# Transposing the sparse heads' attention weights as two 16-bit planes by DMA instead of by TensorE

## The chip, the cores and the metric

The kernel runs on one core of a Trainium2 chip. The metric is the device time of one execution in microseconds (us); below it is better. TensorE (PE) multiplies, VectorE (DVE) and ScalarE (ACT) work on whole tiles, GpSimd (POOL) does the rest, and SyncE (SP) issues most DMAs. Each engine takes its instructions in one fixed order.

## The reference

One layer of a hybrid block on 512 tokens of width 1024: a combined input projection, two attention branches of eight heads each (head size 64), sigmoid gates, an output projection, a layer norm, a gated MLP with a short causal convolution, and a second layer norm, all in float32. The change touches branch A, the sparse one:

```
dots  = einsum('thd,sd->ths', q_idx, k_idx) * IDX_DIM ** -0.5
score = einsum('th,ths->ts', w_idx, relu(dots))           # indexer
_, sel = top_k(where(key_chunk <= q_chunk, score, -inf), n_sel)   # n_sel = 128
logits = einsum('thd,tnhd->htn', qb, k[sel]) * HEAD_DIM ** -0.5 + rel_bias[t5_bucket(sel - t)]
p = softmax(where(valid, logits, -inf))
y_a = einsum('htn,tnhd->thd', p, v[sel])
...
merged = sigmoid(g_a) * (y_a @ w_branch_dsa) + sigmoid(g_b) * (y_s @ w_branch_sb)
```

## The kernel before

Float32 operands are split into a high and a low part of TensorE's own float32 format, and each product is three matmuls (high by high, high by low, low by high). `Stream` loads the weights in one fixed order as pieces of 128x1024 (512 KB, tile `raw`, three buffers) and splits them into `whi` (ACT) and `wlo` (DVE, some on POOL), three pieces ahead of their use.

The kernel's middle part works on 16 heads, first eight stick-breaking ones (s0 to s7), then eight sparse ones (a0 to a7). For each head `start_head` computes logits and weights; a sparse head does that in `dsa_head`. Keys run along the columns there, queries along the 128 partitions; the four query blocks j have 128(j+1) causal keys each, 1280 columns in all, which stand in one tile `lg` at the column offsets `OFF`. TensorE writes the logits to `l_ps`, DVE adds the bias and mask in `bm` and takes a row extreme (L493), ACT takes the exponential with its row sum (L495), DVE multiplies by the reciprocal (L501, four instructions).

The product with the values needs the weights with keys along the partitions. `turn_weights` does that: ten transposes of 128x128 per head on TensorE (L409, into `tr_ps`), then three copies on ACT to the high part `pth` (L413) and three subtractions on DVE to the low part `ptl` (L414). `weigh` multiplies these by the values in eight matmuls (L425, into `av_ps`); `avt`, `yat` and, for each pair of heads, `ya0h`/`ya0l` to `ya3h`/`ya3l` follow. Head i+1 is started before the weights of head i are turned. In the gaps `fill` puts the matmuls of projections that nothing waits for soon (`FILL`: the queries and keys of later heads, the gates `gb` and `ga`, the branch `bs`). One piece of 128x1024 gives 24 such matmuls. After the last head comes branch A's projection (`ba_ps`, L653 to L655), which needs `ya0` to `ya3`.

The written order is not the order on the engines: a scheduler places each instruction, from its own estimate of durations and what has been written first. Pools name a tag and its buffers; a tile waits until the one that had its buffer before has been read. `lg` has two buffers (tag `beta`, shared with the stick-breaking heads), `bm` two (tag `keep`), `pth` and `ptl` eight together (tag `pt`, shared with the indexer's tiles).

Of the kernel before, what the change touches and what calls it, by code (L numbers as in the profile page):

```python
# [21 lines left out]
NB = 4  # L22
# [94 lines left out]
def tile_block(ctx: ExitStack, tc: tile.TileContext, xT, xN, w_qi, w_ki, w_t, w_v, w_br, w_o, w_fi, w_fo,  # L117
# [226 lines left out]
    def idx_keys():  # L344
        ps = whole(proj_t("ki", M=72, bank=pa))
        kih = bp.tile([128, 512], F32R, tag="pt", bufs=8, name="kih")
        kil = bp.tile([128, 512], F32R, tag="pt", bufs=8, name="kil")
        wiT = bp.tile([8, 512], F32, tag="pt", bufs=8, name="wiT")
# [48 lines left out]


    def turn_weights(a):

        groups = (((0, 0),), ((1, 0), (3, 384)), ((2, 0),))
        pth, ptl = {}, {}
        for grp in groups:
            ps = pb("tr_ps")
            width = 0
            for i, o in grp:
# [3 lines left out]
                width = max(width, o + 512 - 128 * i)  # L410
            th = bp.tile([128, 512], F32R, tag="pt", bufs=8, name="pth")
            tl = bp.tile([128, 512], F32R, tag="pt", bufs=8, name="ptl")
            nc.scalar.activation(th[:, :width], ps[:, :width], AF.Copy)  # L413
            lows = nc.vector.tensor_sub(tl[:, :width], ps[:, :width], r32(th[:, :width]))  # L414
            for i, o in grp:
                pth[i] = th[:, o:o + 512 - 128 * i]
                ptl[i] = tl[:, o:o + 512 - 128 * i]
        return pth, ptl, lows.ins

    def weigh(pth, ptl, vt, h, ytmp):  # L420

        ps = pb("av_ps")
        seq = [(i, t) for i in range(NB) for t in (pth, ptl)]
        for n, (i, t) in enumerate(seq):
            nc.tensor.matmul(ps[:, 128 * i:512], vt[i][:, h].rearrange("p a d -> p (a d)"), t[i],  # L425
                             start=(n == 0), stop=(n == len(seq) - 1))
# [44 lines left out]
    def dsa_head(q, k, h):  # L471
# [4 lines left out]
        for j in (1, 2, 3):  # L476
            N = 128 * (j + 1)
            nc.gpsimd.tensor_add(bm[:, OFF[j]:OFF[j] + N], win[:, 512 - N:512], score[j])  # L478
        lg = bp.tile([128, ATT], F32, tag="beta", bufs=2, name="lg")
# [3 lines left out]
        for grp in ((3,), (0, 2), (1,)):  # L483
            ps = pb("l_ps")
            o = 0
            for j in grp:
                N = 128 * (j + 1)
                for hl in range(2):
                    nc.tensor.matmul(ps[:, o:o + N], q[:, hl, j * 128:j * 128 + 128], k[:, :N],
                                     start=(hl == 0), stop=(hl == 1))  # L490
                c = slice(OFF[j], OFF[j] + N)
                b = win[:, 384:512] if j == 0 else bm[:, c]
# [6 lines left out]
        for j in range(NB):  # L499
            c = slice(OFF[j], OFF[j] + 128 * (j + 1))  # L500
            nc.vector.tensor_scalar(lg[:, c], lg[:, c], rs[:, j:j + 1], None, op0=ALU.mult)  # L501
        return lg

# [81 lines left out]
    def start_head(i):  # L585
# [522 lines left out]
```

## Time and profile before

| | us |
|---|---|
| three runs | 764.51, 765.06, 765.46 |
| their median | 765.06 |
| span of the profiled execution | 765.6 |

The span runs from the first to the last instruction of the profiled execution. It is the only time that we have of that execution, and lies 0.5 us above the median. In the page, PE, DVE, ACT and POOL are the engines' busy times in the span, and the chain says which work ended last, followed back from the end. A row of the timeline has the start, the duration, the engine, the line and the operation; since matmuls are pipelined, what one costs is read from the distance of its start to the next start, not from its duration. A row of the groups has the count, the sum of the busy time and the mean of one, then the idle time just before and what ended it.

### The profile page before, as it was taken

To read this page: it belongs to the slowest core of one execution; us is meant where nothing else is said; L and a number is where in the kernel's file an instruction comes from. 1 tells how busy PE (TensorE), PEld (TensorE's weight loads), DVE (VectorE), ACT (ScalarE), POOL (GpSimd) and SP (SyncE) were. 2 spreads that over 40 slices of the span, in tenths; PEclk is the share of its full clock that TensorE was granted. 3 is DMA by queue.
4 is the path that set the end of the run, shared out by engine and by line. 5 is a ranking of instruction groups with operands and counts; after the bars stand their busy time and mean duration, and the time that the engine had idled before them with its cause. 6 is when DMAs were issued, how large, how long until landed. Compare 5 with 4: busy or idle time off the path is not lost.

```text
span 765.6 us, 9873 instructions
## 1 busy us (share of the span) xinstructions
PE 753.1 (98%) x3597; PEld 630.9 (82%) x3597; DVE 555.2 (73%) x908; ACT 365.0 (48%) x559; POOL 153.6 (20%) x160
## 2 busy tenths in 40 slices
PE   8999999999999999999999999999999999999995
PEld 6878888888888888888889888888888888888885
DVE  4559787799878585549855776867676758668994
ACT  5465656655474746836322434433443443346430
POOL 0002546426645210000101110111011101110021
PEclk9999999999999999999999999999999999999998
DMA  7436332232133323116801343433434443447641
GB/s 255 156 110 190 115 111 83 83 95 98 69 111 107 114 72 123 67 58 218 330 1 56 114 162 139 153 144 143 138 139 141 156 140 124 152 137 274 200 155 59
DMA packets 34112, 101.31 MB, mean 132 GB/s; under 512 B 4552, under 2 KB 4936, under 8 KB 34064
## 3 DMA queue, kind: packets, MB, share of 16 engines
q1 hardware_dynamic: 28336, 84.41, 31.6%
q0 software_dynamic: 3728, 11.04, 3.9%
q10 hardware_dynamic: 2000, 5.24, 2.7%
q8 instruction: 28, 0.46, 0.2%
q14 instruction: 20, 0.16, 0.1%
HBM read 88.59 MB, written 9.98 MB: 129 GB/s over the span
## 4 chain that ended last, share of the span: by engine, by line
PE 92%; DVE 5%; issue 1%; ACT 1%; DMA 1%; POOL 0%; POOLq 0%; SPq 0%; ACTq 0%; DVEq 0%
PE u_ps L746 5%; PE u_ps L747 5%; PE g_ps L746 5%; PE u_ps L745 5%; PE g_ps L747 5%; PE g_ps L745 5%; PE m L826 2%; PE m L825 2%; PE m L827 2%; PE av_ps L425 2%; PE ga_ps L223 2%; PE ga_ps L222 2%; PE ga_ps L224 2%; PE o_ps L703 2%; PE o_ps L702 2%; PE o_ps L704 2%
## 5 line engine op out<-in xcount | busy, mean ns | idle before, releaser
L100 ACT ACTIVATE whi<-raw 128x1024 fp32r<-128x1024 f32 (+1 forms) x124 | 124.1, 1001 | 169.5 <-PE g_ps L746 43.0
L102 DVE TENSOR_TENSOR wlo<-raw,whi 128x1024 fp32r<-128x1024 f32 (+1 forms) x105 | 120.0, 1143 | 44.0 <-ACT whi L100 41.1
L745 PE MATMUL u_ps<-x1h,whi 128*128 128x512 f32 (+1 forms) x192 | 71.4, 372 | 0.0
L747 PE MATMUL u_ps<-x1h,wlo 128*128 128x512 f32 (+1 forms) x192 | 71.4, 372 | 0.0
L746 PE MATMUL u_ps<-x1l,whi 128*128 128x512 f32 (+1 forms) x192 | 71.3, 371 | 0.0
L745 PE MATMUL g_ps<-x1h,whi 128*128 128x512 f32 (+1 forms) x184 | 69.9, 380 | 0.0
L746 PE MATMUL g_ps<-x1l,whi 128*128 128x512 f32 (+1 forms) x184 | 69.9, 380 | 0.0
L747 PE MATMUL g_ps<-x1h,wlo 128*128 128x512 f32 (+1 forms) x184 | 69.9, 380 | 0.0
L102 POOL TENSOR_TENSOR wlo<-raw,whi 128x1024 fp32r<-128x1024 f32 x19 | 45.8, 2412 | 34.4 <-ACT whi L100 34.4
L745 PEld LDWEIGHTS u_ps<-x1h,whi 128*128 128x128 f32 x192 | 36.2, 188 | 6.3
L746 PEld LDWEIGHTS u_ps<-x1l,whi 128*128 128x128 f32 x192 | 36.2, 188 | 6.2
L747 PEld LDWEIGHTS u_ps<-x1h,wlo 128*128 128x128 f32 x192 | 36.2, 188 | 6.2
L414 DVE TENSOR_TENSOR ptl<-tr_ps,pth 128x512 fp32r<-128x512 f32 (+1 forms) x48 | 27.9, 595 | 18.2 <-ACT pth L413 17.6
L745 PEld LDWEIGHTS g_ps<-x1h,whi 128*128 128x128 f32 x184 | 34.6, 188 | 6.6
L746 PEld LDWEIGHTS g_ps<-x1l,whi 128*128 128x128 f32 x184 | 34.6, 188 | 6.5
L747 PEld LDWEIGHTS g_ps<-x1h,wlo 128*128 128x128 f32 x184 | 34.6, 188 | 6.5
L768 DVE TENSOR_TENSOR t<-raw 128x512 f32<-128x512 f32 x11 | 7.6, 692 | 39.0 <-DMA raw<-in_w_fo_dram 39.0
L787 POOL MEMSET u<- 128x2 f32 x22 | 2.1, 98 | 150.5 <-ACT whi L100 99.5
L801 DVE TENSOR_TENSOR hF<-g_ps,c 128x512 f32<-128x512 f32 x22 | 15.1, 687 | 19.7 <-PE g_ps L747 18.9
L793 ACT ACTIVATE c<-c,cwt 128x512 f32<-128x512 f32 x22 | 15.9, 725 | 27.9 <-DVE c L792 27.7
L671 POOL TENSOR_TENSOR rstd<-rstd,mhalf 128x1 f32<-128x1 f32 x8 | 7.6, 951 | 105.5 <-DVE rstd L670 105.5
L478 POOL TENSOR_TENSOR bm<-win,score 128x256 f32<-128x256 f32 (+2 forms) x24 | 26.8, 1143 | 9.1 <-DVE mn L493 8.4
(562 smaller groups left out, 2047.9 us busy)
## 6 DMA issues: line engine op xcount, KB each, us to landing
raw<-in_w_fi_dram SPq DMA_DIRECT2D x44, 512.0 KB, 3.2
raw<-in_w_t_dram SPq DMA_DIRECT2D x32, 512.0 KB, 3.3
raw<-in_w_fo_dram SPq DMA_DIRECT2D x26, 512.0 KB, 4.0
raw<-in_w_br_dram SPq DMA_DIRECT2D x8, 512.0 KB, 3.2
raw<-in_w_o_dram SPq DMA_DIRECT2D x8, 512.0 KB, 4.0
raw<-in_w_v_dram SPq DMA_DIRECT2D x7, 512.0 KB, 3.7
raw_b<-in_w_fo_dram SPq DMA_DIRECT2D x6, 512.0 KB, 5.2
s_t<-t POOLq DMA_DIRECT2D x11, 256.0 KB, 2.3
```

Of the source, the lines that this page charges most:

```text
L100: nc.scalar.activation(hi[:, :w], t[:, :w], AF.Copy)
L102: self.done[key] = eng.tensor_sub(lo[:, :w], t[:, :w], r32(hi[:, :w])).ins
L222: nc.tensor.matmul(ps[:M], wh[:, c], xh[k], start=(k == 0), stop=False)
L223: nc.tensor.matmul(ps[:M], wh[:, c], xl[k], start=False, stop=False)
L224: nc.tensor.matmul(ps[:M], wl[:, c], xh[k], start=False, stop=(k == KC - 1))
L414: lows = nc.vector.tensor_sub(tl[:, :width], ps[:, :width], r32(th[:, :width]))
L425: nc.tensor.matmul(ps[:, 128 * i:512], vt[i][:, h].rearrange("p a d -> p (a d)"), t[i], start=(n == 0), stop=(n == len(seq) - 1))
L478: nc.gpsimd.tensor_add(bm[:, OFF[j]:OFF[j] + N], win[:, 512 - N:512], score[j])
L745: nc.tensor.matmul(ps[:, c], wh[:, kc], x1h[:, k, c], start=(k == 0), stop=False)
L746: nc.tensor.matmul(ps[:, c], wh[:, kc], x1l[:, k, c], start=False, stop=False)
L747: nc.tensor.matmul(ps[:, c], wl[:, kc], x1h[:, k, c], start=False, stop=(k == KC - 1))
L793: nc.scalar.activation(c, c, AF.Gelu_apprx_tanh, bias=cwt[:, f, 3:4])
```

## The change

The stick-breaking heads keep `turn_weights`. A sparse head now takes two functions. `send_planes`, called at the end of `dsa_head`, sees each float32 of `lg` as two 16-bit halves: ACT copies the upper halves and DVE the lower halves to two planes of 128x1280, which lie in the head's `bm`, no longer needed by then; SP issues one transposing DMA for each plane into the tile `pl`. `join_planes`, called where `turn_weights` stood, has ACT and DVE write the turned halves back into `lg`, then ACT makes the high part from it and DVE the low part, each in one instruction of 128x1280. The blocks of a sparse head stand at the offsets `SOFF`, so that for each value block the weights lie in 128-column pieces three pieces apart; `weigh` takes ten matmuls for it instead of eight (block 0 is one of 384 columns and one of 128). `pth` and `ptl` are one tile each of 1280 columns for all 16 heads, in one buffer each (tags `th`, `tl`), and `pl` has one buffer. The indexer's tiles, which stood in tag `pt`, use `th`, `tl`, `pl`, and six buffers of `keep`, `av` and `yt`.

```
+SOFF = {1: 0, 0: 256, 2: 384, 3: 768}
...
-                rl = bp.tile([128, 512], F32, tag="pt", bufs=8, name="relu")
+                rl = bp.tile([128, 512], F32, tag=("keep", "av", "yt")[h % 3], bufs=2, name="relu")
...
+    def turned():
+        return (bp.tile([128, ATT], F32R, tag="th", bufs=1, name="pth"),
+                bp.tile([128, ATT], F32R, tag="tl", bufs=1, name="ptl"))
...
+    def halves16(t):
+        return t.bitcast(U16).rearrange("p (c two) -> p two c", two=2)
+
+    def send_planes(lg, bm):
+        src = halves16(lg)
+        own = bm[:, 0:ATT].bitcast(U16).rearrange("p (a c) -> p a c", a=2)
+        pl = bp.tile([128, 2, ATT // 128, 128], U16, tag="pl", bufs=1, name="pl")
+        nc.scalar.activation(own[:, 1], src[:, 1], AF.Copy)
+        nc.vector.tensor_copy(own[:, 0], src[:, 0])
+        for a in (0, 1):
+            nc.sync.dma_start_transpose(pl[:, a], own[:, a])
+        return lg, pl
+
+    def join_planes(lg, pl):
+        raw = halves16(lg)
+        got = pl.rearrange("p a b c -> p a (b c)")
+        nc.scalar.activation(raw[:, 1], got[:, 1], AF.Copy)
+        nc.vector.tensor_copy(raw[:, 0], got[:, 0])
+        th, tl = turned()
+        nc.scalar.activation(th, lg, AF.Copy)
+        lows = nc.vector.tensor_sub(tl, lg, r32(th))
+        h, l = (t.rearrange("p (s c) -> p s c", c=128) for t in (th, tl))
+        parts = [(i, o, h[:, c], l[:, c]) for i, o, c in
+                 ((0, slice(128, 512), slice(0, 9, 3)), (0, slice(0, 128), slice(2, 3)),
+                  (1, slice(128, 512), slice(1, 9, 3)), (2, slice(256, 512), slice(5, 9, 3)),
+                  (3, slice(384, 512), slice(9, 10)))]
+        return parts, lows.ins
...
-        return lg
+        return send_planes(lg, bm) + (None,)
...
-        pth, ptl, lows = turn_weights(weights[0])
+        parts, lows = turn_weights(weights[0]) if w == "s" else join_planes(*weights[:2])
...
-        weigh(pth, ptl, vals[w], h, ytmp)
+        weigh(parts, vals[w], h, ytmp)
```

What the scheduler makes of it is shown at three places. First SP's queue at the end of the sparse heads, before (`win` is the bias window of a head, `raw` a piece of weights):

```order
L70 DMA raw_46_2793<-in_w_t_dram 128x1024
L473 DMA win_2926<-s_win 128x512
L70 DMA raw_47_2840<-in_w_t_dram 128x1024
L473 DMA win_3056<-s_win 128x512
L70 DMA raw_48_2879<-in_w_t_dram 128x1024
```

and now, from the last transposing DMAs of a5 to those of a7:

```order
L438 DMA_TRANSPOSE pl_2657<-bm_2625 128x10x128 x2
L72 DMA raw_49_2829<-in_w_t_dram 128x1024
L72 DMA raw_50_2908<-in_w_t_dram 128x1024
L72 DMA raw_51_2999<-in_w_t_dram 128x1024
L72 DMA raw_52_3038<-in_w_br_dram 128x1024
L72 DMA raw_53_3086<-in_w_br_dram 128x1024
L438 DMA_TRANSPOSE pl_2874<-bm_2842 128x10x128 x2
L72 DMA raw_54_3123<-in_w_br_dram 128x1024
L438 DMA_TRANSPOSE pl_2992<-bm_2960 128x10x128 x2
L72 DMA raw_55_3176<-in_w_br_dram 128x1024
L72 DMA raw_56_3222<-in_w_t_dram 128x1024
```

Loads of weights now stand in one queue behind the transposing DMAs of a6 and a7 (`raw_54` to `raw_56`). Second ACT's queue at the last two heads, before (`pth_3120` and its two followers are a6, `pth_3221` and its followers a7):

```order
L413 ACTIVATE pth_3120<-tr_ps_3115 128x512
L413 ACTIVATE pth_3129<-tr_ps_3124 128x512
L495 ACT_TABLE_LOAD
L495 ACTIVATE lg_3063,sm_3065<-lg_3063,mn_3064 128x384
L413 ACTIVATE pth_3136<-tr_ps_3133 128x256
L100 ACTIVATE whi_52_3153<-raw_52_3151 128x1024
L542 ACTIVATE ga3_3195<-ga3_ps_3157,bgt_105 128x512
L632 ACT_TABLE_LOAD
L632 ACTIVATE ga3_3195<-ga3_3195 128x512
L413 ACTIVATE pth_3221<-tr_ps_3216 128x512
```

and now (`lg_2846`, `bm_2842`, `pl_2874`, `pth_3023` are a6; `lg_2964`, `bm_2960` are a7):

```order
L435 ACTIVATE bm_2842<-lg_2846 128x1280
L102 ACTIVATE whi_51_3001<-raw_51_2999 128x1024
L533 ACTIVATE lg_2964,sm_2966<-lg_2964,mn_2965 128x384
L580 ACTIVATE ga2_3036<-ga2_ps_3005,bgt_105 128x512
L670 ACT_TABLE_LOAD
L670 ACTIVATE ga2_3036<-ga2_3036 128x512
L445 ACTIVATE lg_2846<-pl_2874 128x1280
L448 ACTIVATE pth_3023<-lg_2846 128x1280
L435 ACTIVATE bm_2960<-lg_2964 128x1280
L102 ACTIVATE whi_52_3040<-raw_52_3038 128x1024
```

The copy to a7's plane stands behind a6's joining copy, which waits for a6's DMAs. Third TensorE at the last head, before (the products of a7):

```order
L223 MATMUL ga5_ps_3259<-xl5_303,whi_51_3095 128x512
L425 MATMUL av_ps_3263<-pth_3221,va0_2207 128x512
L425 MATMUL av_ps_3263<-ptl_3222,va0_2207 128x512
L425 MATMUL av_ps_3263<-pth_3230,va1_2210 128x384
L224 MATMUL ga5_ps_3259<-xh5_302,wlo_51_3096 128x512
```

and now:

```order
L226 MATMUL ga5_ps_3129<-xh7_346,wlo_51_3002 128x512
L463 MATMUL av_ps_3133<-pth_3107,va0_2166 128x384
L691 MATMUL ba_ps_3182<-ya0h_2318,whi_52_3040 128x512
L692 MATMUL ba_ps_3182<-ya0l_2319,whi_52_3040 128x512
L693 MATMUL ba_ps_3182<-ya0h_2318,wlo_52_3041 128x512
```

The last filler (`ga5`) is over before a7's first product; in the order before, a part of it still stood behind that product. There are 117 matmuls between the last logits of a6 and a7's first product in the new order.

More of the change, by code (lines that the diff above doesn't have):

```diff
@@ L13 @@
 F32R = mybir.dt.float32r
+U16 = mybir.dt.uint16
 AF = mybir.ActivationFunctionType
@@ L345, in idx_keys @@
         ps = whole(proj_t("ki", M=72, bank=pa))
-        kih = bp.tile([128, 512], F32R, tag="pt", bufs=8, name="kih")
-        kil = bp.tile([128, 512], F32R, tag="pt", bufs=8, name="kil")
-        wiT = bp.tile([8, 512], F32, tag="pt", bufs=8, name="wiT")
+        kih = bp.tile([128, 512], F32R, tag="th", bufs=1, name="kih")
+        kil = bp.tile([128, 512], F32R, tag="tl", bufs=1, name="kil")
+        wiT = bp.tile([8, 512], F32, tag="pl", bufs=1, name="wiT")
         nc.scalar.activation(wiT, ps[64:72], AF.Copy, scale=float(H) ** -0.5)
@@ L396, in select_some @@
             pass
+    def turned():
+        return (bp.tile([128, ATT], F32R, tag="th", bufs=1, name="pth"),
+                bp.tile([128, ATT], F32R, tag="tl", bufs=1, name="ptl"))
     def turn_weights(a):
-        groups = (((0, 0),), ((1, 0), (3, 384)), ((2, 0),))
-        pth, ptl = {}, {}
-        for grp in groups:
+        groups = ((0, ((0, 0),)), (512, ((1, 0), (3, 384))), (1024, ((2, 0),)))
+        th, tl = turned()
+        parts = []
+        for base, grp in groups:
             ps = pb("tr_ps")
@@ L410, in turn_weights @@
                 width = max(width, o + 512 - 128 * i)
[L411 to L414, printed above, removed]
+            w = slice(base, base + width)
+            nc.scalar.activation(th[:, w], ps[:, :width], AF.Copy)
+            lows = nc.vector.tensor_sub(tl[:, w], ps[:, :width], r32(th[:, w]))
@@ L415, in turn_weights @@
             for i, o in grp:
[L416 to L420, printed above, removed]
+                c = slice(base + o, base + o + 512 - 128 * i)
+                parts.append((i, slice(128 * i, 512), th[:, c], tl[:, c]))
+        parts.sort(key=lambda t: t[0])
+        return parts, lows.ins
+    def halves16(t):
+        return t.bitcast(U16).rearrange("p (c two) -> p two c", two=2)
@@ new lines, in send_planes @@
+    def send_planes(lg, bm):
[12 more added lines that the diff above has]
+        nc.vector.tensor_copy(raw[:, 0], got[:, 0])
+        th, tl = turned()
+        nc.scalar.activation(th, lg, AF.Copy)
[5 more added lines that the diff above has]
+                  (3, slice(384, 512), slice(9, 10)))]
+        return parts, lows.ins
@@ L422, in weigh @@
+    def weigh(parts, vt, h, ytmp):
         ps = pb("av_ps")
-        seq = [(i, t) for i in range(NB) for t in (pth, ptl)]
-        for n, (i, t) in enumerate(seq):
-            nc.tensor.matmul(ps[:, 128 * i:512], vt[i][:, h].rearrange("p a d -> p (a d)"), t[i],
+        seq = [(i, o, t) for i, o, th, tl in parts for t in (th, tl)]
+        for n, (i, o, t) in enumerate(seq):
+            dst = ps[:, o] if len(t.shape) == 2 else ps[:, o].rearrange("p (s c) -> p s c", c=128)
+            nc.tensor.matmul(dst, vt[i][:, h].rearrange("p a d -> p (a d)"), t,
@@ L477, in dsa_head @@
             N = 128 * (j + 1)
-            nc.gpsimd.tensor_add(bm[:, OFF[j]:OFF[j] + N], win[:, 512 - N:512], score[j])
+            nc.gpsimd.tensor_add(bm[:, SOFF[j]:SOFF[j] + N], win[:, 512 - N:512], score[j])
         lg = bp.tile([128, ATT], F32, tag="beta", bufs=2, name="lg")
@@ L490, in dsa_head @@
                                      start=(hl == 0), stop=(hl == 1))
-                c = slice(OFF[j], OFF[j] + N)
+                c = slice(SOFF[j], SOFF[j] + N)
                 b = win[:, 384:512] if j == 0 else bm[:, c]
@@ L499, in dsa_head @@
         for j in range(NB):
-            c = slice(OFF[j], OFF[j] + 128 * (j + 1))
+            c = slice(SOFF[j], SOFF[j] + 128 * (j + 1))
             nc.vector.tensor_scalar(lg[:, c], lg[:, c], rs[:, j:j + 1], None, op0=ALU.mult)
-        return lg
+        return send_planes(lg, bm) + (None,)
     def branch(br, key, ys, p, use):
@@ L590, in start_head @@
         args = qk[f"q{w}{h//2}"][h % 2], qk[f"k{w}{h//2}"][h % 2], h
-        return sb_head(*args) if w == "s" else (dsa_head(*args),)
+        return sb_head(*args) if w == "s" else dsa_head(*args)
     weights = start_head(0)
@@ L596, in tile_block @@
     for i, (w, h) in enumerate(heads):
-        following = start_head(i + 1) if i + 1 < len(heads) else (None,)
+        following = start_head(i + 1) if i + 1 < len(heads) else ()
         fill(GAP)
-        pth, ptl, lows = turn_weights(weights[0])
+        parts, lows = turn_weights(weights[0]) if w == "s" else join_planes(*weights[:2])
         if len(following) == 2:
```

## The prediction

> **What bounds the kernel now.** I read the page first, then the busy time by stage, then TensorE's timeline around one block of transposes, then the groups of the other engines.
>
> ```profile
> span 765.6 us, 9873 instructions
> PE 753.1 (98%) x3597; PEld 630.9 (82%) x3597; DVE 555.2 (73%) x908; ACT 365.0 (48%) x559; POOL 153.6 (20%) x160
> PE 92%; DVE 5%; issue 1%; ACT 1%; DMA 1%; POOL 0%; POOLq 0%; SPq 0%; ACTq 0%; DVEq 0%
> ```
>
> TensorE is busy 98% of the span, and 92% of the chain that ended last is its own. By stage (columns: stretch, length, busy time of PE, weight load, DVE, ACT, POOL):
>
> ```profile
> 60.00:93.00 33.00, 33.00 (x151) 27.24 (x150) 29.60 (x74) 18.85 (x34) 12.63 (x11) 1.00 0.44 144
> 93.00:207.00 114.00, 113.06 (x574) 95.41 (x573) 96.47 (x187) 63.92 (x116) 58.47 (x34) 1.00 0.29 95
> 207.00:331.00 124.00, 123.46 (x617) 103.96 (x616) 82.91 (x167) 79.73 (x145) 27.95 (x27) 1.00 0.29 97
> 331.00:380.00 49.00, 49.00 (x217) 40.55 (x217) 38.23 (x50) 24.27 (x29) 2.08 (x3) 1.00 0.59 217
> ```
>
> The sparse heads fill 207 to 331. TensorE idles 0.5 us there and nothing in the 49 us behind it, so each microsecond of matmul taken away there shortens the kernel, as long as nothing new makes TensorE wait. DVE has 41 us free, ACT 44.
>
> **What goes: the transposes.** TensorE in the sparse heads, one block of four transposes, and further down the end of a head's products:
>
> ```profile
> 256.69 0.60 PE L409 MATMUL tr_ps<-ident,lg 128*128 128x128 f32 x4
> 257.05 0.48 PE L224 MATMUL gb_ps<-xh,wlo 128*128 128x512 f32 x1
> 257.36 0.40 PE L222 MATMUL gb_ps<-xh,whi 128*128 128x512 f32 x1
> 257.59 0.39 PE L223 MATMUL gb_ps<-xl,whi 128*128 128x512 f32 x1
> ...
> 269.58 0.28 PE L425 MATMUL av_ps<-ptl,va 128*128 128x256 f32 x1
> 269.70 0.22 PE L425 MATMUL av_ps<-pth,va 128*128 128x128 f32 x1
> 269.76 0.28 PE L425 MATMUL av_ps<-ptl,va 128*128 128x128 f32 x1
> 269.88 0.67 PE L489 MATMUL l_ps<-ka2b,qa2b 128*128 128x128 f32 x4
> ```
>
> What counts is the distance between starts. Four transposes take 257.05 - 256.69 = 0.36, and the matmul behind them 0.31 where its like takes 0.23 (257.59 - 257.36): 0.44 us for four, 0.11 each.
>
> ```profile
> L409 PE MATMUL tr_ps<-ident,lg 128*128 128x128 f32 x80 | 12.3, 272 | 0.0
> ```
>
> 80 x 0.11 = 8.8 us go from TensorE. (The busy sum of 12.3 counts overlap.) Two matmuls of 128 columns more per head come in, with the columns taken from the two of 512: a pair of 128 takes 269.88 - 269.70 = 0.18, the 256 columns saved are 0.12, so 8 x 0.06 = 0.5 us. Net: -8.3 us.
>
> **What comes on ACT and DVE.** Per head, three copies and three subtractions go, three passes of 1280 columns come on each:
>
> ```profile
> L413 ACT ACTIVATE pth<-tr_ps 128x512 fp32r<-128x512 f32 x16 | 9.4, 591 | 1.9 <-PE tr_ps L409 1.8
> L413 ACT ACTIVATE pth<-tr_ps 128x256 fp32r<-128x256 f32 x8 | 3.0, 373 | 0.0
> L100 ACT ACTIVATE whi<-raw 128x1024 fp32r<-128x1024 f32 x19 | 20.1, 1056 | 23.3 <-PE ga_ps L223 6.7 <-PE qa_ps L223 5.3 <-issue 4.6
> L414 DVE TENSOR_TENSOR ptl<-tr_ps,pth 128x512 fp32r<-128x512 f32 x16 | 10.9, 686 | 5.6 <-ACT pth L413 5.5
> L414 DVE TENSOR_TENSOR ptl<-tr_ps,pth 128x256 fp32r<-128x256 f32 x8 | 3.3, 411 | 0.1
> L102 DVE TENSOR_TENSOR wlo<-raw,whi 128x1024 fp32r<-128x1024 f32 x16 | 19.6, 1222 | 13.2 <-ACT whi L100 13.2
> ```
>
> From 512 to 1024 columns ACT adds 0.465, DVE 0.536 us; so 1280 columns are estimated at 1.29 on ACT and 1.49 on DVE. ACT: 3 x 1.29 - (2 x 0.59 + 0.37) = +2.3 per head, 19 us in all, 79.7 to 98 of 116 us. DVE: 3 x 1.49 - (2 x 0.69 + 0.41) = +2.7, 21 us in all, 82.9 to 104 of 116 us, or 90%. In the stage ahead DVE is at 96.5 of 114, 85%, and TensorE idles 0.9. So this work is taken as hidden by TensorE's projections; what it costs without that cover comes below as waiting. No 16-bit copy stands in the trace; its ends are the plain rate (1.49) and, for DVE, these two quartets over the same 1280 columns (L501):
>
> ```profile
> 240.41 5.50 DVE L501 TENSOR_SCALAR lg<-lg,rs 128x128 f32<-128x128 f32 x4
> ...
> 305.80 1.27 DVE L501 TENSOR_SCALAR lg<-lg,rs 128x128 f32<-128x128 f32 x4
> ```
>
> ```profile
> 239.69 3.46 POOL L478 TENSOR_TENSOR bm<-win,score 128x256 f32<-128x256 f32 x3
> 243.10 2.53 POOL L102 TENSOR_TENSOR wlo<-raw,whi 128x1024 fp32r<-128x1024 f32 x1
> ```
>
> The one that took 5.50 ran while POOL was adding, and ended with it. So a copy on DVE lies between 1.27 and 5.5; I take 1.49, since POOL works 28 of 124 us.
>
> **The transposing DMA.** 128 x 1280 x 2 bytes are 320 KB, SBUF to SBUF. No row shows one. The nearest:
>
> ```profile
> qa2b<-qa2b ACTq DMA_DIRECT2D x1, 256.0 KB, 2.9
> qa3a<-qa3a ACTq DMA_DIRECT2D x1, 256.0 KB, 4.6
> raw<-in_w_t_dram SPq DMA_DIRECT2D x32, 512.0 KB, 3.3
> bgt<-in_bg_dram SPq DMA_DIRECT2D x1, 8.0 KB, 2.0
> r<-in_xN_dram SPq DMA_DIRECT2D x4, 512.0 KB, 8.0
> ```
>
> Call the time from the second plane's copy to its landing X. The lower end is 2.0 us (hardly any data), the upper 8.0 (four large DMAs issued at once). I take 3.5, by the plain copies SBUF to SBUF of nearly that size.
>
> **Does TensorE have to wait?** A sparse head's weights now take a longer way, and all engines are in order. I follow the last pair, a6 and a7, where the projections run out, from a6's last logits (t = 0). Rows that it uses:
>
> ```profile
> L493 DVE CUSTOM_DVE_ANT_0 lg<-l_ps,bm 128x384 f32<-128x384 f32 x7 | 3.9, 553 | 5.6 <-PE l_ps L489 5.5
> L495 ACT ACTIVATE lg<-lg,mn 128x384 f32<-128x384 f32 x7 | 4.3, 621 | 0.9 <-DVE mn L493 0.8
> L495 ACT ACT_TABLE_LOAD x5 | 6.4, 1283 | 0.1
> L542 ACT ACTIVATE ga<-ga_ps,bgt 128x512 f32<-128x512 f32 x4 | 2.6, 677 | 0.0
> L632 ACT ACTIVATE ga<-ga 128x512 f32<-128x512 f32 x4 | 2.4, 627 | 0.0
> ```
>
> ACT: a6's exponential 0.6 to 1.4 (with its sum), two of a7, two table loads and a gate to 6.1, one more exponential to 6.8, then a6's plane to 8.1; with X, its DMA has landed at 11.6. Meanwhile ACT splits a weight, does a7's last exponential and another gate with its table, until 12.6. The DMA is thus 1.0 us early. Join 13.9, high part 15.2. TensorE reaches a6's product at about 17.6: a margin of 2.4. Then a7: plane until 16.5, landed 20.0, join 21.3, a weight 22.4, high part 23.7. TensorE reaches a7's product after 117 matmuls, 99 of 0.227 (512 columns) and 18 shorter ones with 2.5 us in sum: 25.0. The margin is 1.3 us. For an earlier head, followed the same way at a4, it is about 3.8.
>
> So with d = X - 3.5 TensorE waits about d + max(0, d - 1) - 1.3 at the last head, since a7's plane stands on ACT behind a6's join and pays twice, and d - 3.8 at each of the seven others, neither below nothing. At 3.5 it waits for nothing; at 7.6 all 8.3 us are spent (5.9 + 2); at 8.0 it waits 6.7 + 7 x 0.7 = 11.6.
>
> **The rest, each with its cover.** On SP the transposing DMAs stand ahead of weight loads and wait for both copies. A piece feeds 24 matmuls, 24 x 0.227 = 5.4 us, and loads run three pieces ahead, so a load may be some 10 us late; the pieces behind a7's (`raw_55`, `raw_56`) are used more than 10 us after its products. If that cover goes, the delay is one of the 3.3 us loads. `pl` in one buffer is the wait already in the chain (a7's DMA after a6's join). `th` and `tl` in one buffer: the next high part waits for the last product of the head before, which stands ahead of it on TensorE anyhow (about 20 in the chain above, ahead of 22.4); uncovered, one 0.59 copy per head. `bm` stays taken until the DMAs land, so POOL adds the bias of head n+2 later; two heads are some 25 us. The indexer has six buffers for its results where it had eight shared with three that stay. The order of blocks moves no work. All of these at zero.
>
> **Sum.** The profiled execution's span, 765.6, stands 0.5 above the median of 765.06; I subtract from the median. 765.06 - 8.8 + 0.5 = 756.8. I add what POOL's holding up a copy costs on average: a copy that takes 5.5 adds at most 4.2 us to a chain, 2.9 beyond the margin of the last head or 0.4 beyond that of another, and POOL works 28 of 124 us, 0.23: 0.23 x (2.9 + 7 x 0.4) = 1.3. Forecast 758.1, and 755 to 761.5 if this is the way it goes.
>
> **Rivals.**
> *DVE's copies are held up by POOL in every head.* 4.2 - 3.8 = 0.4 at seven heads and 4.2 - 1.3 = 2.9 at the last is 5.7, less than the saving: 762.5. For it: POOL's 28 us of bias adds now overlap longer chains. Against: only some of the quartets L501 are slow.
>
> *TensorE waits for the transposing DMA* (slower than before). It decides from X = 7.6. At the row of 8.0 it gives 756.8 + 11.6 = 768.4; at 10 us 756.8 + 10.7 + 7 x 2.7 = 786. For it: two such DMAs are issued together among 512 KB loads, and the row of 8.0 shows what a queue does. Against: SP has only 0.29 of DMA time in use in this stage.
>
> *The DMA goes block by block*, ten blocks one after the other at the trace's smallest round trip: 10 x 2.0 = 20 us each, 40 per head on one queue, 320 us where the stage has 116: about 757 + 204 = 961. For it, no row; against, all DMAs of 128 partitions here move far more per us.
>
> [...]
>
> **How the numbers follow.** A run of this kernel can tell about 0.2% (1.5 us) from no change. Forecast way, 755 to 761.5: 0.57. Copies held up, 761.5 to 763.5: 0.11. X near 7.5, within 0.2%: 0.08. TensorE waits more, 766.6 to 785: 0.17. Block by block: 0.07. So faster 0.68, same 0.08, slower 0.24. The range leaves out block by block, the upper third of the waiting cases (beyond 775) and a few in a hundred below: 755 to 775.
>
> **What will show it.** No `tr_ps` of a sparse head, TensorE with no idle time ahead of `av_ps`, and the stage shorter by 8 us. X is read from the DMA issues of `pl`. If I am wrong on X, TensorE's idle time ahead of `av_ps` names ACT or DVE's high and low parts, which in turn wait on `pl`, and the last head is the worst. If POOL is the cause, DVE's copies show several us against 1.3 to 1.5. If the weights are late, TensorE waits on `whi` or `wlo` with SP behind a transposing DMA.

## The result, and the profile after

The changed kernel takes 774.97 us (median of 4 runs, 774.28 to 776.82), beside 765.12 for the kernel before (4 runs, 764.51 to 765.46): 1.013 of its time, 95% interval 1.0118 to 1.0143. It is 9.9 us slower; 758.1 had been forecast, and a range of 755 to 775.

The page of the changed kernel, its first lines:

```profile
span 773.7 us, 9790 instructions
PE 750.7 (97%) x3533; PEld 627.1 (81%) x3533; DVE 573.7 (74%) x908; ACT 385.6 (50%) x559; POOL 160.6 (21%) x160
PE   9999999997989799999999999999999999999995
PEclk9999999999989999999999999999999999999998
```

TensorE's busy time fell from 753.1 to 750.7 only, and idle time came in: the digits 7, 8 and 7 in its row are slices of 19 us. The clock row, all nines before up to the last slice, has an 8. The stretch from the middle of the stick-breaking heads to behind the last sparse one holds all of it (length, busy time of PE, weight load, DVE, ACT, POOL, then the clock, DMA share and GB/s). Before:

```profile
90.00:345.00 255.00, 253.52 (x1263) 213.40 (x1262) 187.71 (x363) 151.14 (x271) 89.01 (x64) 1.00 0.28 92
```

After:

```profile
90.00:345.00 255.00, 242.85 (x1160) 203.28 (x1159) 200.32 (x354) 167.33 (x264) 94.98 (x63) 0.97 0.42 112
345.00:740.00 395.00, 395.00 (x1829) 330.41 (x1828) 285.68 (x384) 162.11 (x200) 42.14 (x63) 1.00 0.45 152
```

TensorE idles 12.15 us there (255 - 242.85) where it idled 1.48. From 345 to 740 it never stops. What it waits for, after (us in total, times, longest):

```profile
PE l_ps L527 <- DVE ka2a L318: 4.3, 1, 4.3
PE va_ps L245 <- DVE ka1b L319: 4.2, 1, 4.2
PE gb_ps L224 <- DVE va L254: 3.0, 1, 3.0
...
PE av_ps L463 <- DVE ptl L449: 0.3, 1, 0.3
```

Three single waits, none of them for a turned weight; `av_ps`, which the prediction watched, has 0.3. I call the three stall A (`va_ps`, at 189 us, still in the stick-breaking heads), B (`gb_ps`, at 216) and C (`l_ps`, at 264). The stretches behind their starts, in the changed kernel, in windows of 3 us (length, PE busy, clock, DMA share, GB/s):

```profile
192.00:195.00 3.00, 1.76 (x6) 0.85 0.04 16
195.00:198.00 3.00, 3.00 (x10) 0.58 0.00 0
...
216.00:219.00 3.00, 0.04 (x1) 0.83 0.82 262
219.00:222.00 3.00, 2.96 (x7) 0.50 0.03 11
222.00:225.00 3.00, 3.00 (x8) 0.53 0.00 0
...
267.00:270.00 3.00, 1.45 (x7) 0.87 0.78 314
270.00:273.00 3.00, 2.75 (x10) 0.56 0.00 0
```

Each stall is paid twice: the idle time, and then 3.4 us (A, C) or 6.8 us (B, the first microsecond of it still idle) at half the clock; a window of 3 us that lies over an edge shows the mean. A window's loss by the clock is its busy time times what the clock lacks: A 1.76 x 0.15 + 3.00 x 0.42 = 1.5, B 0.04 x 0.17 + 2.96 x 0.50 + 3.00 x 0.47 = 2.9, C 1.45 x 0.13 + 2.75 x 0.44 = 1.4, together 5.8. So 10.7 us more idle time, 5.8 by the clock, less the 8.3 of the forecast saving: +8.2. The spans differ by 773.7 - 765.6 = 8.1, the medians by 9.9. I call this sum, idle time and clock in 90 to 345 against the kernel before, the account of a kernel. (The span before lies 0.5 above the median of its runs, the one after 1.7 below the time of its own run, as in all runs that have both, 1.7 to 2.2. So the profiled execution before took itself some 2 us more than the median run: its first matmuls kept the distance of half the clock, 0.43 us for 512 columns, until 9.8 us, those of the changed kernel (0.32 for 384 columns, 0.17 behind it) until 6.3. That 8.2 meets 8.1 is in part luck, and an account is good to about 2 us.)

The terms that the prediction had to estimate, after:

```profile
L445 ACT ACTIVATE lg<-pl 128x1280 uint16<-128x1280 uint16 x8 | 13.3, 1659 | 6.1 <-DMA pl<-bm 6.0
L448 ACT ACTIVATE pth<-lg 128x1280 fp32r<-128x1280 f32 x8 | 10.2, 1271 | 2.7 <-DVE lg L446 2.7
L435 ACT ACTIVATE bm<-lg 128x1280 uint16<-128x1280 uint16 x8 | 10.1, 1267 | 12.9 <-DVE lg L539 5.8 <-POOL wlo L104 4.1 <-issue 3.0
...
L449 DVE TENSOR_TENSOR ptl<-lg,pth 128x1280 fp32r<-128x1280 f32 x8 | 14.7, 1843 | 2.4 <-ACT pth L448 2.4
L446 DVE COPY lg<-pl 128x1280 uint16<-128x1280 uint16 x8 | 8.3, 1039 | 7.8 <-DMA pl<-bm 7.8
L436 DVE COPY bm<-lg 128x1280 uint16<-128x1280 uint16 x8 | 7.1, 884 | 0.1
```

```profile
pl<-bm SPq DMA_TRANSPOSE x16, 3.6
```

Each transposing DMA lands 3.6 us (median) after its own issue; 3.5 had been taken for X. But X runs from the later copy to the landing of both planes, and the two DMAs of a head stand on SP one behind the other, some 1.5 us apart. From the end of the later copy to the second landing the eight heads have 3.4 to 7.5 us, 4.8 in the median.

### The profile page after: what moved, and what is told of

Its sections match the earlier page's. It is cut to its first block, busy times and chain, and to the rows that moved or that the text cites. A ratio compares the mean times of both kernels' runs of the same rounds, so it can differ in the third digit from the quotient of the medians.

```text
span 773.7 us, 9790 instructions
## 1 busy us (share of the span) xinstructions
PE 750.7 (97%) x3533; PEld 627.1 (81%) x3533; DVE 573.7 (74%) x908; ACT 385.6 (50%) x559; POOL 160.6 (21%) x160
## 4 chain that ended last, share of the span: by engine, by line
PE 63%; DVE 3%; DMA 1%; issue 1%; POOL 0%; ACT 0%; POOLq 0%; DVEq 0%
PE u_ps L785 5%; PE u_ps L784 5%; PE g_ps L785 5%; PE u_ps L783 5%; PE g_ps L784 5%; PE g_ps L783 5%; PE m L864 2%; PE m L865 2%; PE m L863 2%; PE ga_ps L224 2%; PE ga_ps L226 2%; PE ga_ps L225 2%; PE o_ps L742 2%; PE o_ps L741 2%; PE o_ps L740 2%; DMA pl<-bm 1%
## 5 line engine op out<-in xcount | busy, mean ns | idle before, releaser
L104 DVE TENSOR_TENSOR wlo<-raw,whi 128x1024 fp32r<-128x1024 f32 (+1 forms) x105 | 122.8, 1170 | 42.1 <-ACT whi L102 41.3
L516 POOL TENSOR_TENSOR bm<-win,score 128x256 f32<-128x256 f32 (+2 forms) x24 | 33.7, 1431 | 33.8 <-DMA pl<-bm 29.3
L224 PE MATMUL gb_ps<-xh,whi 128*128 128x512 f32 x64 | 26.7, 418 | 3.0 <-DVE va L254 3.0
L503 DVE TENSOR_TENSOR_SCAN keep<-keep,first 128x128 f32<-128x128 f32 (+3 forms) x32 | 29.0, 962 | 0.0
```

The source lines that it names most:

```text
L104: self.done[key] = eng.tensor_sub(lo[:, :w], t[:, :w], r32(hi[:, :w])).ins
L224: nc.tensor.matmul(ps[:M], wh[:, c], xh[k], start=(k == 0), stop=False)
L503: scan = nc.vector.tensor_tensor_scan(rev, rev, first[:, 512 - N:512][:, ::-1], 0.0, op0=ALU.mult, op1=ALU.max)
L516: nc.gpsimd.tensor_add(bm[:, SOFF[j]:SOFF[j] + N], win[:, 512 - N:512], score[j])
```

## The experiments

All were run with the kernel before on the same chip. "Theory" in the expectations is mine as it stood then; the theories A, B and C of the later ones are not the stalls A, B and C. e8, e4, k3, k2 and k4 leave a part of the work out of the result, as their expectations say.

| label | what | us | ratio to before, 95% |
|---|---|---|---|
| e1_tensor_turns | change without DMAs: wide tiles, TensorE turns | 778.33 | 1.0156 to 1.0184 |
| f1_gb5_first | change, gb5 ahead of the values | 776.19 | 1.0146 to 1.0181 |
| e4_join_unsent | change, joins don't wait for the DMAs | 769.74 | 1.0046 to 1.0072 |
| e8_no_turn | change, sparse weights not turned | 765.39 | 1.0002 to 1.0021 |
| h2_pieces6 | before, six pieces, relu moved | 765.78 | 0.9996 to 1.0014 |
| k1_pieces | change, stick-breaking heads in pieces | 770.10 | 1.0054 to 1.0079 |
| k3_no_turn | k1, sparse weights not turned | 759.32 | 0.9906 to 0.9933 |
| k2_unsent | k1, joins don't wait for the DMAs | 763.71 | 0.9965 to 0.9986 |
| k4_no_adds | k1 without POOL's bias adds | 766.40 | 1.0002 to 1.0020 |
| k5_later | k1, products 2 us later | 768.12 | 1.0019 to 1.0040 |
| k10_actmult | k1, normalising on ACT | 773.80 | 1.0099 to 1.0127 |
| k9_dvecopies | k1, copies and joins all on DVE | 765.64 | 0.9997 to 1.0014 |
| k7_swap | k10 and k9 together | 763.99 | 0.9976 to 0.9994 |
| k12_dvecopies_bank | k9, gb5 in another bank | 768.80 | 1.0031 to 1.0058 |
| k11_swap_bank | k7, gb5 in another bank | 761.33 | 0.9938 to 0.9963 |

**e1_tensor_turns**

```
-SOFF = {1: 0, 0: 256, 2: 384, 3: 768}
+SOFF = {0: 0, 2: 128, 3: 512, 1: 1024}
-        return send_planes(lg, bm) + (None,)
+        return lg, None, None
-        parts, lows = turn_weights(weights[0]) if w == "s" else join_planes(*weights[:2])
+        parts, lows = turn_weights(weights[0])
```

> The changed kernel, but the sparse heads' weights are transposed by TensorE again, with the blocks in the old order: what is left of the change is where the tiles stand (high and low parts in one wide buffer each, the indexer's tiles in other buffers). TensorE's order up to the first sparse head's transposes is that of the changed kernel. Theory (three stalls of TensorE, each followed by a halved clock; the first, at 189 us, comes from the new placement and not from the transposing DMAs): the stall at 189 is there, 3.3 us more idle and about 1.6 us of clock, so 765.1 + 4.9 = 770.0. Rival 1 (all of the loss is waiting for the transposing DMAs) and rival 2 (all of it is the added work on ScalarE and VectorE): 765.1.

Measured: 778.33. This is the run that decides. With no DMA and every transpose back on TensorE, the kernel is 13.2 us slower than before, and 3.4 slower than the whole change. Stall A is there, and so is B, which I had put down to the joins. Its largest waits:

```profile
PE gb_ps L224 <- DVE va L254: 4.9, 1, 4.9
PE va_ps L245 <- DVE ka1b L319: 4.2, 1, 4.2
```

Its account: 255 - 245.56 = 9.4 us idle, 8.0 more than before, and 5.2 by the clock (by its windows: 2.3 behind A, 2.9 behind B): 13.2, all of the loss.

Stall A, read in the order of instructions: `va` has four accumulators (0 to 3), the fourth in the PSUM bank that the keys `ka1` leave when DVE has drained them. The accumulators of its 96 matmuls, one digit each, in the order on TensorE:

```
before: 000111000111000222222111222000133333333311222333...
e1:     000111000111222222000133333311222333...
after:  000111000111222222000133333311222333...
```

Thirty-one matmuls stand ahead of the first 3 before, twenty-two now: 9 x 0.227 = 2.0 us less cover. The wait grew by 4.2 - 0.9 = 3.3 us; the rest is on DVE. The drains of `ka1` end 10.3 us after the first matmul of `va` before and 11.6 us in e1, and 1.1 of these 1.3 us are the scan of a stick-breaking head that stands ahead of them, before and in e1:

```profile
185.95 3.98 DVE L465 TENSOR_TENSOR_SCAN keep<-keep,first 128x128 f32<-128x128 f32 x4
```

```profile
184.83 5.11 DVE L503 TENSOR_TENSOR_SCAN keep<-keep,first 128x128 f32<-128x128 f32 x4
```

In e1 a whole split of POOL (2.68 us from 185.60) falls beside it, as in the changed kernel (2.67 us from 186.75, beside a scan of 5.11 from 185.98), before only the second half of one (2.41 us from 184.70). Stall B, DVE's timeline in e1:

```profile
217.57 2.93 DVE L539 TENSOR_SCALAR lg<-lg,rs 128x128 f32<-128x128 f32 x4
220.43 0.41 DVE L420 TENSOR_TENSOR ptl<-tr_ps,pth 128x256 fp32r<-128x256 f32 x1
220.76 1.87 DVE L254 TENSOR_TENSOR va<-va_ps,va 128x512 fp32r<-128x512 f32 x3
```

`gb5` needs a bank that the values hold, and their drains (L254) stand behind a sparse head's normalising products (L539), which take 2.93 us while POOL adds beside them (`bm`, 216.73 to 219.63) and 1.27 alone. In the whole change the same place looks so on DVE:

```profile
216.81 0.89 DVE L446 COPY lg<-pl 128x1280 uint16<-128x1280 uint16 x1 [1.10 <-DMA pl<-bm]
...
218.21 1.28 DVE L254 TENSOR_TENSOR va<-va_ps,va 128x512 fp32r<-128x512 f32 x2
```

There it is a join waiting for its DMA that stands ahead. I had read this as the cause; e1 shows that the stall comes without it. Stall C, in the whole change, has no such place in e1 (DVE, and the two DMAs on SP's queue):

```profile
253.66 4.34 DVE L539 TENSOR_SCALAR lg<-lg,rs 128x128 f32<-128x128 f32 x4
...
259.38 5.01 SPq L438 DMA_TRANSPOSE pl<-bm  x2
...
266.90 0.88 DVE L446 COPY lg<-pl 128x1280 uint16<-128x1280 uint16 x1 [3.87 <-DMA pl<-bm]
267.81 0.68 DVE L318 TENSOR_TENSOR ka2a<-ka_ps,ka2a 64x512 fp32r<-64x512 f32 x1
```

The keys `ka2a`, for which `l_ps` of head a4 waits, stand behind a3's join, which waits 3.87 us for a landing that is late twice over: a3's products took 4.34 us, where 1.27 is usual, and from the end of the copies (259.35) to the join 7.5 us passed, of which the two DMAs took 5.0 us on SP's queue, where those of other heads take 2.9 to 3.8; the second landed 5.8 us after its issue, the longest of the sixteen.

**e8_no_turn and e4_join_unsent**

```
-        return send_planes(lg, bm) + (None,)
+        return lg, None, None
-        raw = halves16(lg)
-        got = pl.rearrange("p a b c -> p a (b c)")
-        nc.scalar.activation(raw[:, 1], got[:, 1], AF.Copy)
-        nc.vector.tensor_copy(raw[:, 0], got[:, 0])
```

> The changed kernel without any transposition in the sparse heads: no 16-bit copies, no transposing DMAs, no joins; high and low parts are taken from the weights as they are. This leaves the transposition of the sparse heads out of the computation. Theory: the 8.3 us that TensorE saves are there, the stalls at 217 and 264 are gone, that at 189 stays: 765.1 - 8.3 + 4.9 = 761.7. Rivals 1 and 2: 765.1 - 8.3 = 756.8. If the saving of 8.3 us were not there: 770.

```
-        return lg, pl
+        return lg, own
-        got = pl.rearrange("p a b c -> p a (b c)")
+        got = pl
```

> The changed kernel, whose joins read the 16-bit planes as they were before the transposing DMAs; copies, joins and DMAs all run, but nothing waits for the DMAs' landing except the next head's DMA. This leaves the transposition out of the result. Theory (the stalls at 217 and 264 are drains that stand behind a join that waits for the DMA): both go, that at 189 stays: about 762. Rival 1 (the DMA wait is all): 757. Rival 2 (the passes on ScalarE and VectorE, not the wait): near 775, as the changed kernel.

Measured: 765.39 and 769.74. Both have A (4.2 us) and, against my theory, B (2.5 and 4.7), with no join that waits. Only C is gone from both. On the wide tiles the saving was eaten before any DMA came into it.

**f1_gb5_first**

```
-FILL = ("... qa1 ka1 va gb5 bs0 bs1 ...
+FILL = ("... qa1 ka1 gb5 va bs0 bs1 ...
```

> The changed kernel, with the projection gb5 ahead of the sparse heads' values in the list of fillers instead of behind them. Theory: at 189 us TensorE reaches the values' fourth accumulator, which needs the bank of the keys ka1, only after gb5, 5.4 us later, when VectorE has long drained it: that stall goes, 775.0 - 4.9 = 770.1, less if the stall at 217 (gb5 needing a bank that the values hold) goes too: 765. Rivals 1 and 2: 775, since neither the DMAs nor the passes change.

Measured: 776.19, no gain. A's wait fell from 4.2 to 2.4 us, but the clock fell all the same, B became a wait of 3.7 of the branch behind the values, and `av_ps` waited 5.6. The wait moved on.

**h2_pieces6**: the kernel before with this, and 6 instead of 8 buffers for all tiles of tag `pt`.

```
-                rl = bp.tile([128, 512], F32, tag="pt", bufs=8, name="relu")
+                rl = bp.tile([128, 512], F32, tag=("keep", "av", "yt")[h % 3], bufs=2, name="relu")
```

> The kernel before, with only two things of the change: the indexer's ReLU results in the other buffers (keep, av, yt), and six buffers of 512 columns for the high and low parts instead of eight, so that a head's parts have no spare buffer, as in the changed kernel, but stand in six separate pieces instead of two wide tiles. Theory (what makes the stalls at 189 and 217 us is the wide tile, whose next use waits for the head's last product, where a piece waits for its own): no stall, 765.1. Rival 1 (the missing spare buffers do it) and rival 2 (the indexer's new buffers do it): as with TensorE's transposes in wide tiles, about 778.

Measured: 765.78, no difference. Neither the missing spare buffers nor the ReLU's places cost anything; TensorE's order in the stick-breaking heads is as before, and so is its busy time in 90 to 345 (253.53). What remains of e1 is the wide tile. My reading, argued and not measured apart: its next use waits until the last product of the head has read it, that of a piece until its own product has, and so the scheduler places the products and what follows them otherwise. (e1 also has the indexer's keys in these tiles; this was not tried apart, but they were last read at 66 us.)

**k1_pieces**

```
+    sp = list(open_pool("sp"))
...
+            th = sp[1].tile([128, 512], F32R, tag="pt", bufs=6, name="pth")
+            tl = sp[1].tile([128, 512], F32R, tag="pt", bufs=6, name="ptl")
...
+        if i == H - 1:
+            close(sp[0])
+            sp[:] = open_pool("ap", reuse_waits="tile")
```

> The changed kernel with its transposing DMAs, but the stick-breaking heads keep six pieces of 512 columns for their high and low parts (in a pool that is closed behind the last of them and gives its place to the two wide tiles of the sparse heads). Theory (the wide tiles cost the stall at 189, and the order of work behind it that leads into the one at 217; the DMAs bring 8.3 us and cost at most the one stall at 264): without the stalls at 189 and 217 it is 765.1 - 8.3 = 756.8, or 756.8 + 5.7 = 762.5 if the stall at 264 comes as before. Rival (the DMAs cause the stalls at 217 and 264 whatever the stage ahead looks like): 756.8 + 5.4 + 5.7 = 767.9.

Measured: 770.10. A is back to 0.9 us, B to 1.1, C to 0.6, as the theory had it, and yet the gain does not come. TensorE's waits:

```profile
PE av_ps L464 <- DVE ptl L450: 3.0, 3, 1.3
PE l_ps L528 <- DVE ka3a L319: 2.0, 1, 2.0
PE av_ps L464 <- ACT pth L449: 1.5, 2, 1.0
```

With the stalls gone, the sparse heads' products come earlier, and now they do wait for their weights. The stalls, it seems, had given that way its slack. One such wait, DVE in k1:

```profile
278.77 0.93 DVE L447 COPY lg<-pl 128x1280 uint16<-128x1280 uint16 x1 [0.94 <-DMA pl<-bm]
279.57 0.69 DVE L556 TENSOR_TENSOR gb<-bs_ps,gb 128x512 f32<-128x512 f32 x1
280.16 3.07 DVE L540 TENSOR_SCALAR lg<-lg,rs 128x128 f32<-128x128 f32 x4
283.15 1.48 DVE L450 TENSOR_TENSOR ptl<-lg,pth 128x1280 fp32r<-128x1280 f32 x1
```

and POOL and TensorE there:

```profile
278.90 3.71 POOL L517 TENSOR_TENSOR bm<-win,score 128x256 f32<-128x256 f32 x3 [5.17 <-DMA pl<-bm]
```

```profile
284.69 0.45 PE L464 MATMUL av_ps<-ptl,va 128*128 128x384 f32 x1 [1.31 <-DVE ptl L450]
```

The landing releases two at once: the join, and POOL's adds, which had waited for `bm`, in which the planes stood; beside POOL the next head's products (L540) take 3.07 us, and the low part stands behind them.

**k3_no_turn, k2_unsent** (the edits of e8 and e4, on k1)

> As k1_pieces, but without any transposition in the sparse heads (no 16-bit copies, DMAs or joins; high and low parts from the weights as they are), which leaves it out of the result. It shows what TensorE's saving of 8.3 us is worth when nothing takes its place: 765.4 - 8.3 = 757.1 if the saving is real and each microsecond of TensorE counts; 770 if k1's loss of 13 us against that lies in the wide tiles of the sparse heads and not in the way to them.

> As k1_pieces, but the joins read the 16-bit planes from where the DMAs take them; copies, joins and DMAs all run, and nobody but the next head's DMA and POOL waits for a landing. This leaves the transposition out of the result. Theory A (k1's waits, 8.7 us more than before and 1.4 us of clock, come from the 3.6 us between copy and landing): most of them go, 770.1 - 8 = 762 or less. Theory B (they come from POOL's bias adds, which slow VectorE's products): they stay, 768 to 771. Theory C (the added passes on ScalarE and VectorE): they stay, 768 to 771.

Measured: 759.32 and 763.71. So 6.0 us are to be had from TensorE when nothing takes the place of its transposes (1.4 of idle time at the values' bank come in, which with them makes 7.4 of the 8.3). The way through copies and DMAs costs k1 770.10 - 759.32 = 10.8: 4.4 are the passes themselves (k2 less k3), 6.4 the waiting for a landing (k1 less k2). Theory A holds for the larger part, C for the rest. (k2's eleven runs spread from 761.3 to 765.2, and each edit gave the scheduler another order, so the split is good to a microsecond or two.)

**k4_no_adds**

```
-            nc.gpsimd.tensor_add(bm[:, SOFF[j]:SOFF[j] + N], win[:, 512 - N:512], score[j])
...
-                b = win[:, 384:512] if j == 0 else bm[:, c]
+                b = win[:, 384:512] if j == 0 else score[j]
```

> As k1_pieces, but POOL's three bias adds of each sparse head are left out, and VectorE adds the index scores alone: the distance bias is left out of the result for three blocks of four. The planes still go through the same buffer. Theory B (VectorE's products L540 took 3.1 us instead of 1.3 beside these adds, ahead of the low part that TensorE waits for; and the adds hold up the next head's copies): the waits go in large part, 763 to 765. Theories A and C: 768 to 771.

Measured: 766.40. The waits ahead of `av_ps` fall from 4.5 to 0.7, as theory B has it, but a stall of 3.9 us at the values' bank, with a clock of 0.50 behind it, takes most of it back. (The profiled execution is the longest of k4's eleven, 2.6 above their median, so that stall need not be in all.) So the adds are part of the cause of those waits; the time alone doesn't show how large a part.

**k5_later**: the `fill` ahead of the product, and the one behind it.

```
-        fill(GAP)
+        fill(GAP if w == "s" else 24)
...
-        fill(GAP)
+        fill(GAP if w == "s" else 6)
```

> As k1_pieces, but in the sparse heads 24 filling matmuls instead of 15 stand between join and product, and 6 instead of 15 behind the product: TensorE comes to the product 9 x 0.227 = 2.0 us later. No work is left out. TensorE's waits ahead of av_ps in k1 are up to 1.3 us each, 4.5 in all. Theory (the margin of the way through the DMA is short by one to two microseconds in most heads): these go, 770.1 - 4.5 - 1.4 of clock = 764.2; the waits of l_ps and gb_ps (4.5 in all) may stay. If instead each delay is carried from head to head, so that 6 matmuls behind the product are too few for the next: 768 to 772.

Measured: 768.12, 2.0 better, but `av_ps` still waits 4.3 us, as if the delays were carried along from head to head. What went is 1.2 us of idle time and the one lowered clock of k1 (1.4).

**k10_actmult, k9_dvecopies, k7_swap**: the first pair of lines is k10's, the other two are k9's, k7 has all three.

```
-            nc.vector.tensor_scalar(lg[:, c], lg[:, c], rs[:, j:j + 1], None, op0=ALU.mult)
+            nc.scalar.activation(lg[:, c], lg[:, c], AF.Copy, scale=rs[:, j:j + 1])
-        nc.scalar.activation(own[:, 1], src[:, 1], AF.Copy)
+        nc.vector.tensor_copy(own[:, 1], src[:, 1])
-        nc.scalar.activation(raw[:, 1], got[:, 1], AF.Copy)
+        nc.vector.tensor_copy(raw[:, 1], got[:, 1])
```

> As k1_pieces, but the normalising products L540 of the sparse heads (lg times rs) are done by ScalarE instead of VectorE; no work is left out. ScalarE gets some 2.2 us per head (by its exponentials over the same columns), VectorE loses 1.3 to 3.1. Theory B (the products of the next head, slowed beside POOL's adds, hold up the low part ahead of which they stand): TensorE's waits for ptl and for ka3a go, 770.1 - 5 = 765. Theory A (it is the landing alone): the way from exponential to copy gets 0.9 us longer and the waits stay or grow, 770 to 774.

> As k1_pieces, but both planes' copies and both joins are done by VectorE (k7_swap without the products on ScalarE); no work is left out. If k7's gain of 6 us over k1 comes from taking the copies and joins off ScalarE, and the products there cost 3.7 as k10 showed over k1: 770.1 - 6.1 - 3.7 = 760 to 764. If the two only work together (VectorE has no room for two more copies while it keeps the products beside POOL's adds): 767 to 771.

> As k10_actmult, and both planes' copies and both joins are done by VectorE instead of one each by ScalarE (a copy measured 0.81 us on VectorE and 1.27 on ScalarE, a join 0.90 and 1.66); no work is left out. Per head ScalarE gets 2.2 - 2.9 = -0.7 us, VectorE 1.7 - 2.0 = -0.3. The copies become 1.6 instead of 1.3 and the joins 1.8 instead of 1.7 long, but they no longer wait for two engines. If what is left over in k10 is one engine's join standing behind other work of ScalarE (table loads of 1.3 us, exponentials): 761 to 764, faster than both kernels. If VectorE's order is the limit (drains behind two joins that wait for a landing): 768 or more.

Measured: 773.80, 765.64 and 763.99. Loading ACT further is worse by 3.7 (`av_ps` waits 6.2 us for its high part); taking the slow 16-bit work off ACT (a copy and a join took 1.27 and 1.66 us there in the changed kernel, 0.88 and 1.04 on DVE) gives 4.5 alone, and 9.8 where the products are on ACT. k9 stands between its two forecasts (760 to 764 and 767 to 771). So the runs point to ACT's queue as the tight place of this way, though ACT is busy only half of the span. Theory B alone is not enough: with the products off DVE (k10) the waits that it names did fall, for `ptl` from 3.0 to 0.7 us and for `ka3a` from 2.0 to 0.4, but the time did not.

**k12_dvecopies_bank, k11_swap_bank**

```
-            ps = yield from proj_t(t)
+            ps = yield from proj_t(t, bank=pb if t == "gb5" else pa)
```

> As k9_dvecopies, with gb5 in the other bank as in k11_swap_bank. Theory: k9's time less the stall at the values' drains, some 3 us where k9 has it. Rival: the same time as k9, because the wait moves on.

> As k7_swap, and the projection gb5 accumulates in one of the four banks that the sparse heads' transposes no longer use, instead of one that the values' drains have to free first; no work is left out. In k7 gb5 waited 1.9 us at 209 and the clock fell to about 0.55 for the 3 us behind it. Theory (each stall costs its idle time and a lower clock behind it): 764.0 - 1.9 - 1.6 = 760.5. Rival (the wait only moves to the next that needs one of the values' banks, the product of the first branch): 763 to 765.

Measured: 768.80 and 761.33. The wait of `gb5` is gone in both. In k12 a wait of 2.7 us for a high part came in elsewhere, and it is 3.2 slower than k9; the traces show 1.2 of this as idle time (6.8 for 5.6 us), and one lowered clock in each. In k11 none came: TensorE idles 4.0 us in the stretch, at full clock:

```profile
90.00:345.00 255.00, 251.00 (x1215) 209.05 (x1214) 203.45 (x350) 167.21 (x288) 94.14 (x63) 1.00 0.42 115
```

k11 leaves no work out and is the fastest of the kernels that don't: 0.995 of the time before (0.9938 to 0.9963), 3.9 us, 13.6 less than the change as it was made. One edit, +3.2 here and -2.7 there: what stands behind it in the order seems to decide.

## Why the prediction was wrong

1. *What goes, -8.3.* Right: k3 has 6.0 in time and 7.4 with its new idle time counted.
2. *What comes on ACT and DVE.* The sizes were good for the high part (1.27 for 1.29) and low for the low part (1.84 in the mean for 1.49, which is the shortest of the eight). DVE's 16-bit copies were quicker than forecast (0.88 and 1.04), ACT's join slower (1.66 for 1.29). That TensorE hides this work, costed at nothing, failed: k2 less k3, 4.4 us.
3. *X, 3.5.* Too low: 4.8 in the median, 3.4 to 7.5. The 3.6 us to landing are as taken, but the sum left out that the second DMA stands behind the first on SP. By the formula this costs next to nothing still: it has a wait from an X of 4.7 on at the last head, where X was 3.4 (4.1 at a6), and from 7.3 on at the others, of which one reached it, with 7.5. "Block by block" is out: a DMA of ten blocks, 320 KB, landed 3.6 us after its issue, where the plain copies of 256 KB before took 2.9 and 4.6.
4. *The rest, all at zero.* **This is the step that failed.** "`th` and `tl` in one buffer: the next high part waits for the last product of the head before, which stands ahead of it on TensorE anyhow (...); uncovered, one 0.59 copy per head." I looked at the sparse heads only. The tiles are shared with the stick-breaking heads, whose order they change; that cost 13.2 us by itself (e1), by A, B and the clock behind them. The row that could have warned is in TensorE's waits before:

```profile
PE va_ps L243 <- DVE ka1b L317: 0.9, 1, 0.9
```

   This place had no cover left before, and the new order has 22 matmuls ahead of it instead of 31. With the stick-breaking heads in their old tiles (k1) the kernel is still at 770.1, 12 above the forecast: that part is what 2 and 5 took as covered.
5. *Margins of 1.3 at the last head and 3.8 at the others.* The risk was looked for in the wrong place: the last pair never waited much, and with the order of before (k1) heads in the middle did. I had followed the chain with the engines free; there the join waits at the head of ACT's and DVE's queues and holds up drains and other heads' products. The landing costs 6.4 us (k1 less k2), with an X of 4.9 at the head of k1 shown above (copies done at 273.81, landed at 278.74), for which the formula gives nothing.
6. *POOL, +1.3.* The slow products are there (at two of eight heads, 2.9 and 4.3 us for 1.27), not for the copies that I had meant but for the products ahead of drains.
7. The time fell in the range of the rival "TensorE waits for the transposing DMA" (768 to 786), whose point of decision, X = 7.6, no head reached; so it was no hit. No rival had the tiles' shape in it, nor the clock, 5.8 us of the 9.9.

Between e1 and the whole change, the DMAs bring 3.4 us; between h2 and k1 they cost 4.3. Both are measured. The likely reason, which no run separates, is that in e1 TensorE's stalls are there already, in whose shadow the longer way is hidden.

Open: what part of the 10.8 us is POOL's, since each edit gave the scheduler another order; and why stall A's place moved by 9 matmuls and not another number, which its estimates decide. For k1 and the kernels made from it the account lies 1 to 3 us below the medians.

## What to carry to other kernels

Where a scheduler places the work, a change of buffers is a change of order for everyone who shares them: look in the new order at the places that have no cover already, in the stages that the change does not mean to touch. A wide tile is held until its last reader is done, pieces each until their own; equal bytes are not equal waits. And when TensorE, which hardly waited before, starts to stall, count what the clock may take behind each stall as well (here 10.7 us of idle time, most of it in three stalls of 3.0 to 4.3 us, and 5.8 by the clock).

## What the runs showed of the hardware

*The clock behind a stall.* Behind A, B and C (3.0 to 4.3 us of waiting) matmuls of 512 columns started every 0.43 us instead of 0.23. Wherever the clock was lowered there in these runs, it stood at exactly half, for 3.41 or 6.83 us, and in each trace the edges of these stretches lay on a grid of 3.41 us, whose place differed from trace to trace. On this grid (length, PE busy, clock, DMA share, GB/s) the window before the fall and the one behind it are, for A, B and C:

```profile
190.70:194.11 3.41, 0.87 (x4) 1.00 0.38 136
194.11:197.53 3.42, 3.42 (x10) 0.50 0.00 0
...
214.59:218.01 3.42, 1.45 (x7) 1.00 0.92 207
218.01:221.42 3.41, 2.38 (x6) 0.50 0.30 121
...
265.79:269.21 3.42, 0.66 (x4) 1.00 1.03 318
269.21:272.62 3.41, 3.16 (x12) 0.50 0.03 13
```

A short stall did not always do it. In k7 a wait of 1.9 us lay in one window, and the clock fell behind it; in e8 2.5 us were shared by two windows, and it did not:

```profile
208.85:212.26 3.41, 1.47 (x7) 1.00 1.03 284
212.26:215.68 3.42, 3.42 (x10) 0.50 0.46 86
```

```profile
213.14:216.55 3.41, 1.62 (x8) 1.00 0.03 11
216.55:219.97 3.42, 2.73 (x13) 1.00 0.44 153
```

Of these windows, the four that had 0.66 to 1.47 us of TensorE's work, and so 1.94 us or more of idle time, were followed by half the clock; those of e8, with 1.79 and 0.69 us idle, were not. So not the length of a stall alone, but how it fell on the grid, went with whether it was paid twice. Executions of one kernel differed too: of k2's eleven, two stand at 761.3 and 761.5 (mean clock 0.997), four at 763.2 to 763.7 (0.995) and five at 764.2 to 765.2 (0.993).

For a sum it is enough that waits of 1.9 us (k7) to 4.9 us (B in e1) cost a second time here, 1.4 to 2.9 us by the clock, which the prediction left out.

*Copies of 16 bits.* 1280 columns into the planes took 0.88 us on DVE and 1.27 on ACT, in the mean of the eight heads, where ACT's float32 pass of 1280 columns (L448) took 1.27 too; out of them, with every second half-word written, 1.04 and 1.66.

*DVE beside POOL.* The normalising products of one head, SBUF to SBUF, took 1.27 us alone (six of the eight heads of the changed kernel), and 2.9 to 4.3 where POOL's adds or splits ran beside a part or all of them (2.86 and 4.34 in the changed kernel, 2.93 and 4.09 in e1, 3.07 in k1).
